# Hyena's filter weights as two diagonal blocks, one matmul for both halves of the positions

## The chip, the cores and the metric

The kernel runs on one core of one Trainium2 chip. The metric is the device time of one execution in microseconds (us). The kernel before takes 1653.63 us, the median of 3 runs that lie between 1647.57 and 1656.79 us.

## The reference, cut to what matters

The program is one layer of an encoder on 1024 positions of width 1024: RMSNorm, a projection whose columns feed four mixers (retention, a Mamba-2 state-space mixer, Hyena, gated DeltaNet), an output projection, a mixture of 16 experts, a gate and a final norm. The change lies in Hyena's long filters. A small network gives each of the L = 1024 positions 64 hidden values; its last layer maps these to 512 channels, 256 of the forward and 256 of the backward filter, and each channel is multiplied with its decay:

```python
def hyena_filters(L, w_in, b_in, w_mid, b_mid, freq, w_out):
    ...
        h = jnp.sin(freq * (h @ w_mid[j] + b_mid[j]))
    h = h @ w_out
    ...
    h = h * (jnp.exp(-t * jnp.abs(deltas)) + HY_SHIFT)
...
f_f = jnp.fft.rfft(filt, n=2 * L, axis=0)
```

The filters then go through a discrete Fourier transform, and the spectra are multiplied with those of the Hyena values.

## The kernel before

**Stages.** The first mixer stage projects the normalised input into the columns of the four mixers (matmuls L318 and L300, issued as fp32 split into a high and a low part), runs the gated DeltaNet's triangular inverses (`gdn_inverse`, VectorE lines L652 and L654 in 30 steps, then one ScalarE copy L657 and a store to DRAM, L658) and its scan (`gdn_scan`), and computes Hyena's filters and their transforms (`hy_transforms`). The scan fetches the stored inverses (L700) before its first matmuls (L714, L717), works on with L731, L744 and L761, and keeps its small evacuations on ScalarE. Later stages hold the other mixers, the output projection and the experts.

**Hyena's filters.** `hid` holds the hidden values (index 0 forward, index 1 mirrored for the backward filter): the 64 of the first half of the positions on partitions 0 to 63, those of the second half on partitions 64 to 127. `hy_transforms` goes through four quarters of 64 channels. In each it loads the weights `wo` (both halves' partitions get the same 64 rows, by GpSimd's queue, L1153), the decay `S` (L1154) and the bias (L1155). Then for each half `h` of the positions it makes eight matmuls with contraction 64 and 64 moved columns into the PSUM tile `tk`, of which there is one buffer, and VectorE multiplies the 128x512 results with the decay (L1166). In fp32 each matmul is issued as two passes, so a half is 16 passes in the trace, a quarter 32, the whole 128. After the second half, GpSimd adds the bias (L1168), forms sum and difference (L1170, L1171), ScalarE copies (L1172), and `dft16` makes a 16-point transform out of GpSimd additions (L1208) and ScalarE scalings (L1209); a store of the spectra (L1175) ends the quarter. A second loop of four quarters loads the Hyena values (L1180), runs `dft16` on them and stores (L1183). All tiles are slices of the two buffers `prm` and `prr`.

**Order.** The generators of these parts are woven into each other:

```python
weave((self.gdn_inverse(), 10), (islice(rest, 40), 40), (islice(tf, 6), 6))
weave((self.gdn_scan(), 48), (rest, 88), (tf, 14))
```

Here `rest` are the remaining projections and `tf` is `hy_transforms`. This is the order in the program's text only: the framework's scheduler, which works from modelled times of each instruction, sets the order in which each engine gets its instructions. The filters' matmuls are held behind the last projection matmul issued so far (`self.after(self.on_pj.ins)`). An engine works through its own list in order. The projections' convolution tile `cin` has its edges cleared by GpSimd (L335, L336), in the same list as the additions of `dft16`.

Of the kernel before, what the change touches and what calls it, by code (L numbers as in the profile page):

```python
# [14 lines left out]
OP = mybir.AluOpType  # L15
# [833 lines left out]
class Mix:  # L849
# [288 lines left out]
    def hy_transforms(self):  # L1138

        nc, a = self.nc, self.a  # L1140
        room = self.t1([128, 2432], "prm")
        z = room[:, 1024:2048].rearrange("p (a b) -> p a b", a=16)
        w = self.t1([128, 768], "prr").rearrange("p (a b) -> p a b", a=12)

        S = room[:, 0:1024].rearrange("p (i t c) -> p i t c", i=2, t=8)
        wo = room[:, 2048:2176].rearrange("p (i c) -> p i c", i=2)
        bi = room[0:1, 2176:2240]
        cols = lambda x: x.rearrange("p (i c) -> p i c", i=2)
        dec = a["c_fdec"].rearrange("(t p) (i c) -> i p t c", p=128, i=2)
        for q in range(4):  # L1150
            qs = slice(q * 64, q * 64 + 64)
            for h in range(2):
                nc.gpsimd.dma_start(wo[h * 64:h * 64 + 64], cols(a["hy_filt_w_out"][0])[:, :, qs])  # L1153
                nc.sync.dma_start(S[:, h], dec[h][:, :, qs])  # L1154
            nc.sync.dma_start(bi, a["hy_bias"][:, qs])  # L1155
            yield
            for h in range(2):
                sl = slice(h * 64, h * 64 + 64)
                ph = self.p([128, 2, 4, 64], "tk", 1)
                with self.after(self.on_pj.ins):  # L1160
                    for t in range(4):
                        for i in range(2):
                            nc.tensor.matmul(ph[:, i, t], lhsT=self.hid[sl, i, t * 128:t * 128 + 128], rhs=wo[sl, i],
                                             start=True, stop=True)
                v = S[:, :, h * 4:h * 4 + 4]
                nc.vector.tensor_tensor(out=v, in0=ph, in1=v, op=OP.mult)  # L1166

            nc.gpsimd.tensor_tensor(out=S[0:1, 0, 0], in0=S[0:1, 0, 0], in1=bi, op=OP.add)  # L1168

            nc.gpsimd.tensor_tensor(out=w[:, 0:8], in0=S[:, 0], in1=S[:, 1], op=OP.add)  # L1170
            nc.gpsimd.tensor_tensor(out=S[:, 1], in0=S[:, 0], in1=S[:, 1], op=OP.subtract)  # L1171
            nc.scalar.copy(S[:, 0], w[:, 0:8])  # L1172
            yield
            self.dft16(S[:, 0], S[:, 1], lambda i: z[:, i], w)
            nc.gpsimd.dma_start(self.ZF[:, :, qs], z)  # L1175
            yield
        for q in range(4):
            qs = slice(q * 64, q * 64 + 64)
            x = room[:, (q % 2) * 512:(q % 2) * 512 + 512].rearrange("p (t c) -> p t c", t=8)
            nc.sync.dma_start(x, self.HV[:, :, qs].rearrange("t p c -> p t c"))  # L1180
            yield
            self.dft16(x, x, lambda i: z[:, i], w)
            nc.sync.dma_start(self.ZX[:, :, qs], z)  # L1183
            yield
# [1059 lines left out]
```

## Time and profile before

| what | value |
|---|---|
| median of 3 runs | 1653.63 us |
| the profiled execution | 1651.48 us |
| its span, first to last instruction | 1649.6 us |
| mean granted TensorE clock | 0.959 |
| TensorE matmuls (PE) busy | 1513.7 us, 92% |
| VectorE (DVE) busy | 1195.3 us, 72% |
| ScalarE (ACT) busy | 862.2 us, 52% |
| GpSimd (POOL) busy | 559.0 us, 34% |
| chain that ended last | PE 45%, DMA 18%, DVE 17%, issue 8%, POOL 6%, ACT 5% |

Busy shares are of the span. The chain is followed back from the last instruction, at each step to what released it. Times in rows count from the span's start, and the profiled execution is 1.9 us longer than its span. A bracket such as `[2.47 <-ACT mo L922]` at the end of a row says how long the engine was idle before the instruction and which instruction ended that. PE is TensorE's matmuls, PEld its weight loads, SP the engine that issues most transfers (SPq is its queue).

### The profile page before, as it was taken

To read this page: it belongs to the slowest core of one execution; us is meant where nothing else is said; L and a number is where in the kernel's file an instruction comes from. 1 tells how busy PE (TensorE), PEld (TensorE's weight loads), DVE (VectorE), ACT (ScalarE), POOL (GpSimd) and SP (SyncE) were. 2 spreads that over 40 slices of the span, in tenths; PEclk is the share of its full clock that TensorE was granted. 3 is DMA by queue.
4 is the path that set the end of the run, shared out by engine and by line. 5 is a ranking of instruction groups with operands and counts; after the bars stand their busy time and mean duration, and the time that the engine had idled before them with its cause. 6 is when DMAs were issued, how large, how long until landed. Compare 5 with 4: busy or idle time off the path is not lost.

```text
span 1649.6 us, 25979 instructions
## 1 busy us (share of the span) xinstructions
PE 1513.7 (92%) x9148; PEld 1251.9 (76%) x9148; DVE 1195.3 (72%) x2060; ACT 862.2 (52%) x1413; POOL 559.0 (34%) x778
## 2 busy tenths in 40 slices
PE   4999999999999899779997999999898999999997
PEld 4877778988778776568875787886676688787886
DVE  5589876942556477955778797998888887777673
ACT  6255342123444335433223776887776767676662
POOL 3126665672865068462223110111111021121121
PEclk9999999999999899869997999999999999999999
DMA  5213557454545485154345999999999988888771
GB/s 182 61 39 96 168 155 243 131 161 105 166 122 167 139 288 163 55 181 156 135 154 214 359 337 363 317 339 350 349 355 336 348 294 295 293 310 303 236 276 52
DMA packets 200671, 362.53 MB, mean 220 GB/s; under 512 B 62046, under 2 KB 124732, under 8 KB 200285
## 3 DMA queue, kind: packets, MB, share of 16 engines
q1 hardware_dynamic: 169016, 296.13, 52.2%
q0 software_dynamic: 12400, 42.29, 8.5%
q10 hardware_dynamic: 19125, 22.45, 4.0%
q8 instruction: 72, 1.18, 0.3%
q14 instruction: 58, 0.48, 0.1%
HBM read 301.04 MB, written 59.77 MB: 219 GB/s over the span
## 4 chain that ended last, share of the span: by engine, by line
PE 45%; DMA 18%; DVE 17%; issue 8%; POOL 6%; ACT 5%; SPq 0%; POOLq 0%; ACTq 0%; DVEq 0%
PE pj L300 8%; DVE wl L1622 6%; PE pj L318 5%; PE ga L1646 4%; DMA raw<-in_exp_w_gate_dram 4%; PE ga L1648 4%; PE ga L1647 4%; DMA raw<-in_exp_w_up_dram 3%; ACT wh L1620 2%; POOL prm L1208 2%; POOL prr L1208 2%; PE pj L1647 2%; PE pj L1646 2%; PE pj L1648 2%; DMA RT<-mo 2%
## 5 line engine op out<-in xcount | busy, mean ns | idle before, releaser
L1622 DVE TENSOR_TENSOR wl<-raw,wh 128x1024 fp32r<-128x1024 f32 x340 | 408.3, 1223 | 86.2 <-ACT wh L1620 83.6
L1620 ACT CAST wh<-raw 128x1024 fp32r<-128x1024 f32 x344 | 356.4, 1052 | 139.1 <-DMA raw<-in_exp_w_up_dram 46.1
L1647 PE MATMUL ga<-wl,xh 128*128 128x512 f32 x512 | 206.4, 403 | 6.8 <-DVE wl L1622 6.7
L1648 PE MATMUL ga<-wh,xl 128*128 128x512 f32 x480 | 189.8, 396 | 0.0
L1646 PE MATMUL ga<-wh,xh 128*128 128x512 f32 x480 | 177.2, 407 | 10.0 <-ACT wh L1620 9.7
L1647 PEld LDWEIGHTS ga<-wl,xh 128*128 128x128 f32 x512 | 98.1, 192 | 34.7 <-DVE wl L1622 15.9
L318 PE MATMUL pj<-wh,hnh 128*128 128x256 f32 (+1 forms) x384 | 113.0, 295 | 7.9 <-DVE zss L915 4.6
L300 PE MATMUL pj<-hnh,wh 128*128 128x512 f32 x288 | 118.4, 411 | 0.8 <-ACT cin L337 0.8
L1646 PEld LDWEIGHTS ga<-wh,xh 128*128 128x128 f32 x480 | 90.6, 191 | 34.9 <-ACT wh L1620 16.5
L300 PE MATMUL pj<-hnl,wh 128*128 128x512 f32 x288 | 117.0, 406 | 0.0
L2009 POOL DMA_INDIRECT H<-b,pidx x15 | 35.4, 2357 | 240.6 <-ACT b L2008 213.7
L300 PE MATMUL pj<-hnh,wl 128*128 128x512 f32 x288 | 116.7, 405 | 0.0
L318 PE MATMUL pj<-wl,hnh 128*128 128x256 f32 (+1 forms) x384 | 110.5, 288 | 0.0
L318 PE MATMUL pj<-wh,hnl 128*128 128x256 f32 (+1 forms) x384 | 110.5, 288 | 0.0
L1647 PE MATMUL pj<-wl,hh 128*128 128x512 f32 x256 | 103.8, 406 | 4.1 <-DVE wl L1622 4.1
L1648 PEld LDWEIGHTS ga<-wh,xl 128*128 128x128 f32 x480 | 91.8, 191 | 18.1
L1648 PE MATMUL pj<-wh,hl 128*128 128x512 f32 x256 | 100.1, 396 | 0.0
L1956 POOL DMA_INDIRECT a<-HN,pidx x16 | 29.9, 1871 | 200.0 <-PE pj L1647 66.4
L1646 PE MATMUL pj<-wh,hh 128*128 128x512 f32 x256 | 89.9, 397 | 0.2 <-ACT hh L1636 0.2
L318 PEld LDWEIGHTS pj<-wh,hnh 128*128 128x128 f32 x384 | 74.4, 194 | 10.4 <-issue 4.1
L346 DVE SCALAR_TENSOR_TENSOR cacc<-cin,pcolh,cacc 128x1024 f32<-128x1024 f32 x48 | 64.8, 1349 | 15.6 <-POOL prm L1208 7.0
L318 PEld LDWEIGHTS pj<-wl,hnh 128*128 128x128 f32 x384 | 74.3, 193 | 0.5 <-issue 0.3
(540 smaller groups left out, 3751.6 us busy)
## 6 DMA issues: line engine op xcount, KB each, us to landing
raw<-in_exp_w_down_dram SPq DMA_DIRECT2D x128, 512.0 KB
raw<-in_exp_w_gate_dram SPq DMA_DIRECT2D x108, 512.0 KB
raw<-in_exp_w_up_dram SPq DMA_DIRECT2D x104, 512.0 KB
wraw<-in_w_in_dram SPq DMA_DIRECT2D x30, 512.0 KB
g<-WD SPq DMA_DIRECT2D x16, 768.0 KB
room<-in_exp_w_up_dram SPq DMA_DIRECT2D x24, 512.0 KB
WD<-gB SPq DMA_DIRECT2D x16, 640.0 KB
room<-in_exp_w_gate_dram SPq DMA_DIRECT2D x18, 512.0 KB
```

The costliest lines, as they stand in the source:

```text
L300: self.on_pj = nc.tensor.matmul(pj, lhsT=A[:, kt], rhs=B[:, kt, hs], start=i == 0, stop=i == 23)
L318: self.on_pj = nc.tensor.matmul(pj, lhsT=A[:, kt, ts], rhs=B[:, kt, :], start=i == 0, stop=i == 23)
L346: nc.vector.scalar_tensor_tensor(acc, cin[:, 2 - r + j:2 - r + j + 1024], w[j], acc, op0=OP.mult, op1=OP.add)
L1208: tt = lambda o, a, b, op: nc.gpsimd.tensor_tensor(out=o, in0=a, in1=b, op=op)
L1620: nc.scalar.copy(h, r)
L1622: e.tensor_tensor(out=l, in0=r, in1=h.bitcast(F32), op=OP.subtract)
L1646: nc.tensor.matmul(ps, lhsT=xh[:, k], rhs=wh[:, hs], start=first, stop=False)
L1647: nc.tensor.matmul(ps, lhsT=xh[:, k], rhs=wl[:, hs], start=False, stop=False)
L1648: return nc.tensor.matmul(ps, lhsT=xl[:, k], rhs=wh[:, hs], start=False, stop=last)
L1956: self.fetched = self.nc.gpsimd.indirect_dma_start(out=xg, out_offset=None, in_=self.HN if src is None else src, in_offset=bass.IndirectOf ...
L2009: nc.gpsimd.indirect_dma_start(out=self.H, out_offset=bass.IndirectOffsetOnAxis(ap=idx[:, :1], axis=0), in_=y, in_offset=None, compute_op= ...
```

## The change

The weights `wo` become two diagonal blocks on 128 partitions: rows 0 to 63 feed the columns of the first half, rows 64 to 127 those of the second, and the off-diagonal blocks are zeroed once by two GpSimd memsets of 64x2x64 (L1152 after the change). A matmul then contracts over all 128 partitions and moves 128 columns, and gives both halves of the positions for 128 positions at once. The loop over the halves `h` becomes one over `n`, the pairs of position tiles: per `n` four matmuls (8 passes) instead of eight (16 passes). The layout of `tk` is one PSUM bank as before; the product with the decay is done in two VectorE operations of 128x2x2x64 (128x256) instead of one of 128x512. Names: L1163 is L1165 after the change, L1166 is L1169; the other lines of the function after them move by 3.

```diff
+        wo = room[:, 2048:2304].rearrange("p (i h c) -> p i h c", i=2, h=2)
+        bi = room[0:1, 2304:2368]
+        for h in range(2):
+            nc.gpsimd.memset(wo[h * 64:h * 64 + 64, :, 1 - h], 0.0)
...
-                nc.gpsimd.dma_start(wo[h * 64:h * 64 + 64], cols(a["hy_filt_w_out"][0])[:, :, qs])
+                nc.gpsimd.dma_start(wo[h * 64:h * 64 + 64, :, h], cols(a["hy_filt_w_out"][0])[:, :, qs])
...
-            for h in range(2):
-                sl = slice(h * 64, h * 64 + 64)
-                ph = self.p([128, 2, 4, 64], "tk", 1)
+            for n in range(2):
+                ph = self.p([128, 2, 2, 2, 64], "tk", 1)
                 with self.after(self.on_pj.ins):
-                    for t in range(4):
+                    for t in range(2):
                         for i in range(2):
-                            nc.tensor.matmul(ph[:, i, t], lhsT=self.hid[sl, i, t * 128:t * 128 + 128], rhs=wo[sl, i],
-                                             start=True, stop=True)
-                v = S[:, :, h * 4:h * 4 + 4]
-                nc.vector.tensor_tensor(out=v, in0=ph, in1=v, op=OP.mult)
+                            nc.tensor.matmul(ph[:, i, t], lhsT=self.hid[:, i, (2 * n + t) * 128:(2 * n + t) * 128 + 128],
+                                             rhs=wo[:, i], start=True, stop=True)
+                v = S.rearrange("p i (h t) c -> p i t h c", h=2)[:, :, 2 * n:2 * n + 2]
+                for i in range(2):
+                    nc.vector.tensor_tensor(out=v[:, i], in0=ph[:, i], in1=v[:, i], op=OP.mult)
```

The scheduler's order moves with it. On VectorE, at the end of the inverses (L652 and L654 are their last steps; L1166 and L1169 the third quarter's products with the decay; L926 a projection's product), the order before was:

```order
L652 TENSOR_TENSOR gB<-gB,g_2541 128x2x30
L654 TENSOR_TENSOR gB<-gB 128x2x30
L285 TENSOR_TENSOR wl<-wraw,wh 128x1024
L1166 TENSOR_TENSOR prm<-tk,prm 128x2x256
L926 SCALAR_TENSOR_TENSOR mo<-zss,pj 128x256
L1166 TENSOR_TENSOR prm<-tk,prm 128x2x256
```

and now it is:

```order
L285 TENSOR_TENSOR wl<-wraw,wh 128x1024
L652 TENSOR_TENSOR gB<-gB,g_2541 128x2x30
L1169 TENSOR_TENSOR prm<-tk,prm 128x2x2x64 x2
L654 TENSOR_TENSOR gB<-gB 128x2x30
L926 SCALAR_TENSOR_TENSOR mo<-zss,pj 128x256
L1169 TENSOR_TENSOR prm<-tk,prm 128x2x2x64 x2
```

The last step of the inverses now stands behind the third quarter's first products, which wait for their matmuls. On ScalarE, the copy of the finished inverses (L657), which the store L658 waits for, stood before among the projections' evacuations (L922, L925) like this:

```order
L922 COPY mo<-pj 128x256
L928 DMA RT<-mo 128x256
L657 COPY gB<-gB 128x32x32
L922 COPY mo<-pj 128x256
L284 CAST wh<-wraw 128x1024
L928 DMA RT<-mo 128x256
L925 ACTIVATE zss<-pj 128x256
```

and now like this:

```order
L922 COPY mo<-pj 128x256
L284 CAST wh<-wraw 128x1024
L928 DMA RT<-mo 128x256
L925 ACTIVATE zss<-pj 128x256
L657 COPY gB<-gB 128x32x32
L928 DMA RT<-mo 128x256
```

The copy has moved behind an evacuation, a cast and the first L925. On TensorE, at the fourth quarter's matmuls in the scan (L1163, L1165 after the change; the L7xx are the scan's, L300 the projections'), the order before was, from the quarter's first matmuls on:

```order
L1163 MATMUL tk<-prm,hid 128x64 x3
L761 MATMUL sp<-gB,g_3419 128x64 x4
L1163 MATMUL tk<-prm,hid 128x64 x2
L714 MATMUL ga<-gB 32x32 x8
L717 MATMUL ga<-gB 32x32
L761 MATMUL sp<-gB,g_3419 128x64 x4
L717 MATMUL ga<-gB 32x32 x7
L1163 MATMUL tk<-prm,hid 128x64 x3
L717 MATMUL ga<-gB 32x32 x8
```

with the second half's matmuls eleven rows further on; now it is:

```order
L1165 MATMUL tk<-prm,hid 128x128 x4
L761 MATMUL sp<-gB,g_3408 128x64 x4
L717 MATMUL ga<-gB 32x32 x16
L761 MATMUL sp<-gB,g_3408 128x64 x4
L1165 MATMUL tk<-prm,hid 128x128 x4
```

The two groups of the quarter, which before were spread over the scan's matmuls and eight projection matmuls, now stand close together.

## Rows read from the trace of the kernel before

**Rows 1.** Busy time by stretch; columns are named in the first line.

```profile
core 0: us, PE busy (x) PEld busy (x) DVE busy (x) ACT busy (x) POOL busy (x), PEclk, DMA share, GB/s
300.00:320.00 20.00, 17.71 (x147) 16.99 (x147) 19.15 (x46) 1.06 (x1) 8.88 (x17) 1.00 0.45 120
340.00:365.00 25.00, 24.92 (x204) 24.17 (x204) 6.35 (x14) 6.20 (x11) 15.37 (x35) 0.94 0.68 222
348.00:353.00 5.00, 5.00 (x42) 4.80 (x42) 2.22 (x3) 1.03 (x2) 0.92 (x2) 1.00 1.02 372
365.00:397.00 32.00, 32.00 (x398) 28.24 (x397) 9.55 (x17) 14.55 (x47) 13.96 (x36) 1.00 0.54 143
440.00:460.00 20.00, 17.87 (x132) 14.92 (x132) 8.97 (x12) 9.00 (x26) 14.92 (x36) 0.91 0.59 168
480.00:500.00 20.00, 16.82 (x155) 13.88 (x154) 8.87 (x12) 8.13 (x24) 15.02 (x33) 0.91 0.36 95
500.00:520.00 20.00, 17.59 (x134) 13.87 (x133) 12.51 (x16) 7.48 (x19) 14.33 (x26) 1.00 0.52 145
```

**Rows 2.** Chain of waits, 330 to 360: start, us, what.

```profile
340.08 8.62 PE pj L318 x60
348.70 1.93 PE tk L1163 x16
350.63 3.38 PE pj L318 x27
354.01 1.93 PE tk L1163 x16
355.93 4.08 PE pj L318 x33
```

**Rows 3.** Line L1163: count, duration ns min/median/max, first and last start.

```profile
L1163 PE MATMUL tk<-prm,hid x128: 272/272/472, 270.4 to 411.1; 64*128 64x64 f32 x128
```

**Rows 4.** Timeline, TensorE, 645 to 655: start, us, engine, line, tiles, count.

```profile
648.60 0.66 PE L1032 MATMUL ga<-sxb 128*128 128x128 f32 x4
649.10 1.03 PE L1035 MATMUL ga<-sST,sxb 128*128 128x256 f32 x4
```

**Rows 5.** Line L1166: count, duration ns min/median/max, first and last start.

```profile
L1166 DVE TENSOR_TENSOR prm<-tk,prm x8: 673/691/692, 275.6 to 411.5; 128x512 f32<-128x512 f32 x8
```

**Rows 6.** Timeline, a VectorE product from PSUM and a GpSimd memset.

```profile
313.38 0.42 DVE L912 TENSOR_TENSOR mo<-pj,rrot 128x256 f32<-128x256 f32 x1 [0.51 <-DMA RT<-mo]
361.60 0.68 POOL L758 MEMSET gB<- 64x256 f32 x2
```

**Rows 7.** Timeline 340 to 372, the inverses' last step, their copy and the scan's start.

```profile
342.35 0.36 DVE L654 TENSOR_TENSOR gB<-gB 128x60 f32<-128x60 f32 x1
345.27 2.09 ACT L657 COPY gB<-gB 128x1024 f32<-128x1024 f32 x1 [0.40 <-ACT mo L922]
347.38 0.32 SPq L658 DMA_DIRECT2D RA<-gB  x1
352.28 0.38 ACT L925 ACTIVATE zss<-pj 128x256 f32<-128x256 f32 x1 [3.63 <-PE pj L318]
358.00 0.35 SPq L700 DMA_DIRECT2D gB<-RU  x1
362.77 0.43 PE L714 MATMUL ga<-gB 32*32 32x32 f32 x8
```

**Rows 8.** Timeline 330 to 345, ScalarE's wait and TensorE's behind it.

```profile
338.20 1.57 ACT L1209 ACTIVATE prr<-prr 128x64 f32<-128x64 f32 x6 [3.74 <-POOL prr L1208]
340.08 0.58 PE L318 MATMUL pj<-wh,hnh 128*128 128x256 f32 x1 [2.47 <-ACT mo L922]
```

**Rows 9.** Timeline 390 to 420, the fourth quarter's matmuls and GpSimd.

```profile
397.10 0.88 PE L1163 MATMUL tk<-prm,hid 64*128 64x64 f32 x6
404.15 0.31 POOL L1168 TENSOR_TENSOR prm<-prm 1x64 f32<-1x64 f32 x1 [19.12 <-DVE prm L1166]
409.42 2.00 PE L1163 MATMUL tk<-prm,hid 64*128 64x64 f32 x16
```

**Rows 10.** Timeline 470 to 530, ScalarE and TensorE in the tail of the scan.

```profile
486.00 0.26 ACT L1209 ACTIVATE prr<-prr 128x64 f32<-128x64 f32 x1 [7.21 <-POOL prr L1208]
491.12 1.14 PE L717 MATMUL ga<-gB 32*32 32x32 f32 x32 [3.18 <-ACT gB L720]
```

More of the change, by code (lines that the diff above doesn't have):

```diff
@@ L1145, in hy_transforms @@
         S = room[:, 0:1024].rearrange("p (i t c) -> p i t c", i=2, t=8)
-        wo = room[:, 2048:2176].rearrange("p (i c) -> p i c", i=2)
-        bi = room[0:1, 2176:2240]
+        wo = room[:, 2048:2304].rearrange("p (i h c) -> p i h c", i=2, h=2)
+        bi = room[0:1, 2304:2368]
         cols = lambda x: x.rearrange("p (i c) -> p i c", i=2)
         dec = a["c_fdec"].rearrange("(t p) (i c) -> i p t c", p=128, i=2)
+        for h in range(2):
+            nc.gpsimd.memset(wo[h * 64:h * 64 + 64, :, 1 - h], 0.0)
         for q in range(4):
```

## The prediction

> **What bounds the kernel now.** I read the shares of the whole span first: TensorE is busy for 92% of it and holds 45% of the chain, so time saved on TensorE can count, but only where TensorE is what ends last. So next the busy time by stretch, over the part that holds the filters. From 300 to 320 VectorE works 19.15 of 20 us and TensorE 17.71: VectorE, with the inverses and the evacuations, is the bound [rows 1]. From 340 to 397 TensorE has 24.92 of 25 and 32.00 of 32 us: it is the bound, and a pass removed there is time [rows 1]. The chain agrees: from 340.08 to past 355.93 it is nothing but projection matmuls and two groups of the filter [rows 2]. In the tail of the scan TensorE idles again: 20 − 17.87, 20 − 16.82 and 20 − 17.59 make 7.7 us, and in two of these stretches the granted clock is 0.91 [rows 1]. The filter's matmuls run from 270.4 to 411.1 in eight groups of 16 passes [rows 3]: four of them by 320, four from 348.70 on [rows 2].
>
> **What goes: half of the passes.** A group of 16 passes with 64 moved columns takes 1.93 us, 0.121 each [rows 2]. The new group has 8 passes of 128x128 weights with 128 moved columns. The same shape runs in the second stage: four passes from 648.60 until the next line starts at 649.10, 0.50 us, or 0.124 each [rows 4]. So a new group should take 8 × 0.124 = 0.99 and saves 0.94. By the busy time of the same row, 0.66 for four, it would be 1.32 and save 0.61. From below, no saving at all (a rival, below). I take 0.94, since the start of the next line is when the engine was free. The four early groups lie where VectorE is the bound, so I count 0 for them (at most −3.8). The four late ones are on the path: 4 × 0.94 = **−3.8** (−2.4 by the dearer price).
>
> **What is added.** VectorE: one product of 128x512 takes 0.69 us [rows 5]; of the new 128x256 ones the nearest row is a product out of PSUM of that size, 0.42 [rows 6]. Two make 0.84, so +0.15 for each of eight, 1.2 in all. The late four are covered by a VectorE that works 6.35 of 25 us and 9.55 of 32 [rows 1]; the early four are not, 0.6. GpSimd: the two memsets of 64x256 at 361.60 took 0.34 each [rows 6]; the new ones write half as much, before the filters' first loads, where nothing of the filter has begun: they cost 0 unless GpSimd is late there, 0.7 if it is. Loads are the same in number and bytes. Together I take **+0.5** (0 to 1.3).
>
> **What is moved: the start of the scan.** Before, the inverses' last step ends at 342.35 + 0.36 = 342.7, their copy runs from 345.27 to 347.4, the store goes out at 347.38, the first fetch at 358.00, and the scan's first matmul is at 362.77 [rows 7]. In the new order on VectorE the last L654 stands behind the third quarter's products, which wait for a group that TensorE began at 348.70 [rows 2]. On ScalarE the copy now stands behind the first L925, which waited 3.63 us for its projection and began at 352.28 [rows 7]. With one group 0.94 shorter ahead of it, L925 begins at 351.3 and ends at 351.7, and the copy ends at 353.8. (The last L654 is done by then: group at 348.70 + 0.99, 0.84 for the products, 0.36, so 350.9.) The store is thus 353.8 − 347.4 = 6.4 us later than before. Behind the copy in ScalarE's list stand the transfers and evacuations of the projections, 2.09 us each time they are due in that moment; two PSUM buffers cover that.
>
> What does TensorE do meanwhile? The order gives it 26 more projection matmuls before the scan's first one. Such matmuls take 4.08/33 = 0.124 [rows 2], so 3.2 us; two shorter groups give back 1.9. It comes to the scan's first matmul at 362.77 + 3.2 − 1.9 = 364.1. The fetched inverses: before, it took 358.00 − 347.38 = 10.6 us from the store to the first fetch, and 4.8 more to the matmul [rows 7]. If both stay, the data is there at 353.8 + 15.4 = 369.2, and TensorE waits 5.1. But the store went out into a stretch where the transfers' share was 1.02, their engines full [rows 1]; later it competes with fewer, and with 6 instead of 10.6 the wait is 0.5. Between 0.5 and 5.1 I take **+3**, nearer to the row than to the hope.
>
> **What is moved: the second quarter.** Before 340.08 TensorE idled 2.47 us for an evacuation by ScalarE, which had itself waited 3.74 us for GpSimd's additions of the transform [rows 8]. VectorE now reaches the second quarter's last product two places earlier in its list, so these additions start earlier. The wait goes, or stays: between −2.5 and 0, and I take **−1**; the same chain of GpSimd and ScalarE is the next thing late there.
>
> **What is moved: the fourth quarter.** Before, its matmuls began at 397.10 and the second group ended at 409.42 + 2.00 = 411.4, with the scan's matmuls and eight projections in between; GpSimd idled 19.12 us for the first product and could form the sum only after the second [rows 9]. Now both groups stand together, so that GpSimd begins up to 411.4 − 397.1 − 3 = some 11 us earlier (3 us for the two groups and the scan's matmuls between them). GpSimd's transforms are late in the tail: there ScalarE stands 7.21 us behind the additions (L1209 waits for L1208), and TensorE 3.18 for an evacuation that ScalarE owes the scan [rows 10]. If that goes, TensorE wins the 7.7 us of idle time and what the clock lost: 0.91 over 20 us is 1.8 us lost in each of two stretches (the mean between the level of 2.4 GHz and that of 1.2, after TensorE had paused), 3.6 in all. So between 0 and −11.3. But the scaling stays ahead of the scan's evacuations in ScalarE's list, the transforms of the second loop keep their number, and the scan itself starts later, so the collision is shifted more than removed. I take **−3**, a quarter.
>
> **Sum.** −3.8 + 0.5 + 3 − 1 − 3 = −4.3. The profiled execution took 1651.5 us, which gives 1647.2. The median of the runs shown is 2.1 above it, so I forecast 1653.6 − 4.3 = **1649.3**. All later stages stand as before, since their instructions are the same.
>
> **Rivals.**
> B, the tail is freed: the early fourth quarter takes all of the 11.3 away. For it: the idle time of GpSimd before 404.15. Against it: the same additions, in the same number, still compete for ScalarE. −3.8 + 0.5 + 3 − 1 − 11.3 = −12.6, so 1641.0.
>
> C, the scan waits, and the kernel is slower: the copy behind the first L925 makes TensorE wait the whole 5.1 us at the scan's first matmul. After that pause the clock falls as in the tail, 1.8 more, and the next fetches are late by 0.9 (between the scan's first groups now stand seven projection matmuls fewer, 7 × 0.124). Nothing is won at the second quarter or in the tail. −3.8 + 0.5 + 5.1 + 1.8 + 0.9 = +4.5, so 1658.1; with waits in the tail that grow by as much as the start is late, up to 1664. For it: the orders on both engines, and a path that in the rows took 15.4 us. Against: the full queues at that moment. It decides against me once store to fetch takes 9 us or more.
>
> D, no saving on TensorE: the time of a pass goes with its moved columns, so that 8 × 128 cost what 16 × 64 did. Then −3.8 falls away: −0.5, so 1653.1. Against it: 0.121 at 64 columns and 0.124 at 128 [rows 2, 4]. The Trainium skill ("TensorE: Matmul & The Clock Gate", section "Back-to-back issue gap") has a rule of this kind: its table gives about 60 cycles for a matmul of up to 64 moved columns and 134 for one of 128, so that by an estimate from it 16 passes cost 960 cycles and 8 cost 1072, and the change would win nothing. Rows 2 and 4 of this case differ from it: the passes stand 0.121 and 0.124 us apart, far over both figures. The same page ("LDWEIGHTS (loading the stationary operand)") says that a weight load takes its time by its columns and not by the contraction, by which the fuller contraction is free; the trace agrees in so far as the pass with all 128 rows is no dearer.
>
> **How the numbers follow.** Chances: forecast 0.47, B 0.23, C 0.25, D 0.05. The forecast's own range is 1641 to 1658, from its bounds (tail −8 to 0, start +0.5 to +5.1). What this measurement can tell from no change is about 0.5%, 8.3 us: faster is below 1645.4, slower above 1661.9. Faster: 0.12 of the forecast's 0.47, 0.18 of B = 0.30. Slower: 0.01 of the forecast, 0.14 of C (its upper half), 0.01 of D = 0.16. The rest, 0.54, is no difference that can be told. The range reaches over most of B and C: 1637 to 1663.
>
> **What would show it.** The group of L1165 takes 1.0 us, not 1.9 (else D). The store of the inverses goes out near 353.8; the first L714 starts near 364 to 369 with TensorE idle 0.5 to 5 before it (over 5: C). The fourth quarter's sum on GpSimd starts near 401 instead of 412.33. Idle time of TensorE from 440 to 520 is 4 to 7 us and one of the dips of the clock is gone (none left: B). The forecast fails if the scheduler's other moves, in the convolution tiles and the second stage, cost or save more than these terms.

## The result: 1% faster, past the forecast

The changed kernel takes 1635.7 us (median of 6 runs, 1632.0 to 1641.3); the kernel before, on the same chip, 1653.3. The ratio is 0.990, 95% interval 0.9875 to 0.992, so some 17.5 us faster. The forecast was 1649.3 with a range of 1637 to 1663. The profiled executions are 1631.96 and 1651.48, the spans 1630.1 and 1649.6.

Nearly all of it is won in one place. Three parts of the first mixer stage, cut at the same projection matmuls in both kernels (the 793rd, the 1301st, and the 1537th, which is the first L300 of the last group), show it; the third part ends with the scan's last matmul. The kernel before, busy time by stretch:

```profile
core 0: us, PE busy (x) PEld busy (x) DVE busy (x) ACT busy (x) POOL busy (x), PEclk, DMA share, GB/s
255.60:341.10 85.50, 76.07 (x597) 73.40 (x597) 71.97 (x156) 17.10 (x37) 53.77 (x82) 0.95 0.56 171
341.10:383.10 42.00, 42.00 (x438) 39.80 (x438) 10.12 (x20) 14.50 (x39) 27.58 (x67) 0.98 0.63 185
383.10:564.20 181.10, 173.14 (x1629) 148.60 (x1627) 91.50 (x125) 73.29 (x190) 85.37 (x172) 0.96 0.44 125
```

The kernel after:

```profile
254.40:338.80 84.40, 71.94 (x565) 69.85 (x566) 68.89 (x152) 16.69 (x37) 52.79 (x82) 0.94 0.58 172
338.80:381.10 42.30, 39.52 (x366) 37.15 (x365) 10.45 (x26) 12.90 (x34) 29.13 (x69) 0.92 0.58 168
381.10:547.00 165.90, 165.66 (x1667) 142.84 (x1667) 94.75 (x131) 75.52 (x197) 72.14 (x172) 1.00 0.51 141
```

The first two parts hold six of the eight filter groups, and they take 127.5 us before and 126.7 after, a gain of only 0.8 us. TensorE does have less to do there: its busy time, less what the slow clock costs, falls from 113.0 to 102.9 us, by 48 passes and by 56 small matmuls of the scan, which now come behind the third cut (168 of the scan's stand ahead of it before, 112 after). But its idle time grows from 9.4 to 15.2 us, and the slow clock costs 8.5 us instead of 5.1. The third part, the tail of the scan, falls from 181.1 to 165.9 us. Before, TensorE idled 8.0 us in it and ran 13.7 us of it at 1.2 GHz, which costs 6.8 by an estimate (half of that time; the last section has the rows at either clock); after, it idles 0.2 us and the granted clock is 1.00 throughout. That is 14.5 of the 15.2.

The same numbers can be summed by kind and not by place: of the 16.0 us that the three parts win, 10.7 are work that is gone (the passes some 8 of it, by an estimate from 8 groups of 1.93 − 0.89), 1.9 idle time and 3.4 slow clock. So the saved work turns into waiting ahead of the tail, and in the tail waiting goes; what each would be worth alone is the question of the experiments.

From the end of the stage to the end of the run the kernel after takes 2.3 us less (1083.1 and 1085.4). Over the profiles of all fourteen kernels here that rest lies between 1081 and 1096 us, so I read nothing from the difference.

The terms one by one. Lines L1165 and L1169 (count, duration min/median/max, first and last start):

```profile
L1165 PE MATMUL tk<-prm,hid x64: 270/275/348, 269.5 to 394.2; 128*128 128x128 f32 x64
L1169 DVE TENSOR_TENSOR prm<-tk,prm x16: 406/416/426, 271.6 to 394.9; 128x256 f32<-128x256 f32 x16
```

The two new memsets, and TensorE's wait at the second quarter:

```profile
L1152 POOL MEMSET prm<- x2: 198/200/202, 262.8 to 263.0; 64x128 f32 x2
338.25 0.38 PE L318 MATMUL pj<-wh,hnh 128*128 128x256 f32 x1 [2.91 <-ACT mo L922]
```

The scan's start, by the chain of waits (start, us, what) and the timeline:

```profile
345.33 0.89 PE tk L1165 x8
346.22 1.43 PE pj L318 x12
347.65 0.02 issue
347.68 0.05 ACT zss L925
347.73 0.23 issue
347.96 2.10 ACT gB L657
350.06 0.02 issue
350.08 10.90 DMA RA<-gB
```

```profile
347.40 0.27 DVE L654 TENSOR_TENSOR gB<-gB 128x60 f32<-128x60 f32 x1
363.40 0.41 PE L714 MATMUL ga<-gB 32*32 32x32 f32 x8 [1.12 <-DMA gB<-RA]
```

On the chain a group now takes 0.89 instead of the 1.93 of [rows 2]. The last L654 ends at 347.7 instead of 342.7, the copy stands behind the first L925 as the order said, and TensorE waits 1.12 us at the scan's first matmul [rows 7]. In the tail, GpSimd's sum of the fourth quarter in the kernel before:

```profile
412.33 1.28 POOL L1170 TENSOR_TENSOR prr<-prm 128x512 f32<-128x512 f32 x1 [7.86 <-issue]
```

And the timeline of the kernel after on TensorE, GpSimd and ScalarE:

```profile
389.79 1.05 PE L1165 MATMUL tk<-prm,hid 128*128 128x128 f32 x8
393.37 1.11 PE L1165 MATMUL tk<-prm,hid 128*128 128x128 f32 x8
395.41 1.27 POOL L1173 TENSOR_TENSOR prr<-prm 128x512 f32<-128x512 f32 x1 [3.72 <-issue]
478.80 0.54 ACT L1212 ACTIVATE prr<-prr 128x64 f32<-128x64 f32 x2 [4.13 <-POOL prr L1211]
```

The fourth quarter's sum starts 17 us earlier (395.41 instead of 412.33), and ScalarE's longest wait for the additions falls from 7.21 [rows 10] to 4.13. In the kernel before, TensorE's waits in the tail ended mostly with ScalarE's evacuations (who waited for what; us in total, times, longest):

```profile
PE ga L717 <- ACT gB L720: 3.2, 1, 3.2
PE sp L761 <- DVE g L748: 2.4, 2, 1.4
PE ga L744 <- ACT gB L732: 2.1, 1, 2.1
```

In the kernel after only a wait of 0.2 is left. The last store of the second loop goes out at 490.7 instead of 522.4, so the chain of transforms has gained 31 us, 14 more than TensorE. What waits in SP's queue between 400 and 530 shows a second list that changes. Before:

```profile
SPq L1183 <- POOL prm L1208: 16.5, 2, 13.4
SPq L1180 <- POOL prr L1208: 10.0, 2, 8.6
SPq L1183 <- POOL cin L336: 8.9, 1, 8.9
```

After:

```profile
SPq L1186 <- POOL prm L1211: 8.0, 3, 3.4
SPq L1183 <- POOL prr L1211: 5.4, 3, 3.0
```

The store of a spectrum (L1183, L1186 after the change) or the load of the next values (L1180, now L1183) waits for GpSimd at the head of SP's queue, and behind it stand the scan's fetches (L700, L693) and the projections' weights (L282). Before, it held them up to 13.4 us at a time, now 3.4. That this list cost TensorE time in the kernel before is not shown: the rows above name ScalarE and VectorE. The prediction had read ScalarE's list in the tail, not SP's.

### The profile page after: what moved, and what is told of

It reads as the page before. It is cut to its first block, busy times and chain, and to the rows that moved or that the text cites. A ratio compares the mean times of both kernels' runs of the same rounds, so it can differ in the third digit from the quotient of the medians.

```text
span 1630.1 us, 25864 instructions
## 1 busy us (share of the span) xinstructions
PE 1494.8 (92%) x9084; PEld 1235.3 (76%) x9084; DVE 1200.2 (74%) x2068; ACT 860.4 (53%) x1413; POOL 558.2 (34%) x780
## 4 chain that ended last, share of the span: by engine, by line
PE 50%; DMA 19%; DVE 16%; issue 7%; ACT 5%; POOL 3%; SPq 0%; POOLq 0%; ACTq 0%; DVEq 0%
PE pj L300 12%; DVE wl L1625 5%; PE pj L318 5%; DMA raw<-in_exp_w_gate_dram 5%; PE ga L1649 5%; PE ga L1651 5%; PE ga L1650 5%; DMA raw<-in_exp_w_up_dram 3%; ACT wh L1623 2%; PE pj L1650 2%; PE pj L1651 2%; PE pj L1649 2%; PE sp L761 2%; DMA a<-H,tidx 1%; DMA raw<-in_exp_w_down_dram 1%
## 5 line engine op out<-in xcount | busy, mean ns | idle before, releaser
L318 PE MATMUL pj<-wh,hnh 128*128 128x256 f32 (+1 forms) x384 | 113.7, 297 | 13.4 <-DVE zss L915 8.6
L2012 POOL DMA_INDIRECT H<-b,pidx x15 | 39.3, 2617 | 238.4 <-ACT b L2011 169.0
L300 PE MATMUL pj<-hnh,wh 128*128 128x512 f32 x288 | 116.7, 405 | 0.8 <-ACT cin L337 0.8
L300 PE MATMUL pj<-hnh,wl 128*128 128x512 f32 x288 | 115.7, 402 | 0.0
L300 PE MATMUL pj<-hnl,wh 128*128 128x512 f32 x288 | 115.7, 402 | 0.0
L1959 POOL DMA_INDIRECT a<-HN,pidx x16 | 37.6, 2349 | 187.4 <-PE pj L1650 65.5
L318 PEld LDWEIGHTS pj<-wh,hnl 128*128 128x128 f32 x384 | 75.1, 196 | 0.7 <-issue 0.5
```

The costliest lines, as they stand in the source:

```text
L300: self.on_pj = nc.tensor.matmul(pj, lhsT=A[:, kt], rhs=B[:, kt, hs], start=i == 0, stop=i == 23)
L318: self.on_pj = nc.tensor.matmul(pj, lhsT=A[:, kt, ts], rhs=B[:, kt, :], start=i == 0, stop=i == 23)
L1959: self.fetched = self.nc.gpsimd.indirect_dma_start(out=xg, out_offset=None, in_=self.HN if src is None else src, in_offset=bass.IndirectOf ...
L2012: nc.gpsimd.indirect_dma_start(out=self.H, out_offset=bass.IndirectOffsetOnAxis(ap=idx[:, :1], axis=0), in_=y, in_offset=None, compute_op= ...
```

## The experiments

"Tail" is the part from the first L300 of the last group to the last scan matmul; its idle time and its loss to the clock (half of the time that the trace puts at 1.2 GHz) are from one profile each, the times from all runs, and ratios are to the kernel before on the same chip. The cut lies between 379 and 387 us, but at 393 in x1 and at 401 in x6, since more of the scan stands ahead of it there.

| kernel | median us | ratio, 95% | tail: idle + clock us | last store of spectra |
|---|---|---|---|---|
| before | 1651 to 1657 | 1 | 8.0 + 6.8 | 522 |
| after | 1635.7 | 0.990, 0.9875 to 0.992 | 0.2 + 0 | 491 |
| x1_two_products | 1657.2 | 1.0015, 1.000 to 1.003 | 7.8 + 3.4 | 521 |
| x2_one_product | 1639.5 | 0.991, 0.988 to 0.994 | 0.2 + 0 | 496 |
| x3_twice | 1649.4 | 0.997, 0.995 to 1.000 | 4.6 + 5.1 | 516 |
| x6_weave | 1647.0 | 0.996, 0.994 to 0.998 | 3.7 + 3.4 | 499 |
| x5_later4 | 1645.1 | 0.993, 0.9905 to 0.996 | 3.9 + 1.7 | 530 |
| x9_no_second | 1636.2 | 0.989, 0.9865 to 0.992 | 0.2 + 3.4 | 467 |
| x14_after_no_second | 1638.1 | 0.9885, 0.9855 to 0.991 | 0.2 + 0 | 455 |
| x10_inverse_first | 1645.5 | 0.994, 0.992 to 0.996 | 5.0 + 1.7 | 495 |
| x11_after_weave | 1644.4 | 0.993, 0.991 to 0.995 | 2.1 + 3.4 | 492 |
| x7_scale_pool | 1663.9 | 1.006, 1.0035 to 1.008 | 14.1 + 10.2 | 531 |
| x13_pool_queue | 1674.8 | 1.012, 1.009 to 1.014 | 13.9 + 20.5 | 552 |
| x15_three_cut | 1650.1 | 0.999, 0.998 to 1.000 | 0.2 + 6.8 | 545 |

**Which part of the change does it: x1, x2, x3.** In x1 the kernel before gets only the split product:

```diff
-                nc.vector.tensor_tensor(out=v, in0=ph, in1=v, op=OP.mult)
+                for i in range(2):
+                    nc.vector.tensor_tensor(out=v[:, i], in0=ph[:, i], in1=v[:, i], op=OP.mult)
```

> The kernel before with only VectorE's side of the change: two products of 128x256 per half instead of one of 128x512; matmuls as before. Theory (half the passes, and an earlier fourth quarter that frees the tail of the scan): nothing is gained, 1653 within 5, TensorE's idle time and slow clock from 400 to 520 stay at some 14 us together. Rival 1 (the split products and the order they bring free the tail): 1645 or less.

Measured: 1657.2, ratio 1.0015, idle time and slow clock of the tail 11.2 (a stretch of slow clock near 401, 3.4 in the kernel before, is missing). Nothing is gained, as the theory says. In x2 the kernel after loses the split and keeps the diagonal blocks:

```diff
-                            nc.tensor.matmul(ph[:, i, t], lhsT=...
+                            nc.tensor.matmul(ph[:, i, :, t], lhsT=...
...
-                v = S.rearrange("p i (h t) c -> p i t h c", h=2)[:, :, 2 * n:2 * n + 2]
-                for i in range(2):
-                    nc.vector.tensor_tensor(out=v[:, i], in0=ph[:, i], in1=v[:, i], op=OP.mult)
+                v = S.rearrange("p i (h t) c -> p (i h) (t c)", h=2)[:, :, 128 * n:128 * n + 128]
+                nc.vector.tensor_tensor(out=v, in0=ph.rearrange("p i h t c -> p (i h) (t c)"), in1=v, op=OP.mult)
```

> The kernel after with VectorE's split undone: the block-diagonal matmuls write PSUM in strides, and one product of 128x512 follows. Theory: the tail stays free, 1636 within 5, VectorE about 1 us less busy. Rival 1 (the split products free the tail): back to 1645 to 1650.

Measured: 1639.5, tail free. Rival 1 falls. In x3 every block-diagonal matmul is issued twice:

```diff
-                            nc.tensor.matmul(ph[:, i, t], lhsT=...
+                            for _ in range(2):
+                                nc.tensor.matmul(ph[:, i, t], lhsT=...
```

> The kernel after with each block-diagonal matmul issued twice, so that a group is 16 passes again (some 1.98 us); loads, products and layout as after. Theory: the passes' 4 to 8 us come back, the fourth quarter's groups are spread over the scan's matmuls again, and the tail idles again: 1648 to 1654. Rival 1 (grouping and products matter, not the passes): the tail stays free, only the passes come back, 1640 to 1645.

Measured: 1649.4, the last groups spread out again in the order, 9.7 us of idle time and slow clock back. So the gain goes with the length of the groups. As x3 also puts back the passes, some 8 us, it does not by itself divide the passes from the tail.

**Does an early fourth quarter free the tail: x6 and x5.** x6 is the kernel before with a larger share for the transforms in the weave:

```diff
-        weave((self.gdn_scan(), 48), (rest, 88), (tf, 14))
+        weave((self.gdn_scan(), 48), (rest, 88), (tf, 18))
```

> The kernel before, all its passes kept, with the transforms given a larger share in the second weave (18 instead of 14), so that the fourth quarter comes earlier in the program. Theory: the transforms end before the scan's evacuations need ScalarE, idle time and slow clock from 400 to 520 fall from 14 us to under 5, 1640 to 1646. Rival 2 (only the removed passes count, and what the tail lost was given by chance): no change, 1650 to 1656.

Measured: 1647.0, a ratio of 0.996, and 7.1 us left in the tail. Another 5.1 us of slow clock, from 388 to 398, lie just ahead of the cut of x6; with them 12.2 of 14.8 us are left, so that the idle time is halved and the slow clock has not shrunk. The direction of the theory, then, and less than half its size. With every pass kept, an earlier start alone gains 0.2 to 0.6%. x5 is the reverse, the kernel after with its fourth quarter held back:

```diff
             yield
+            if q == 3:
+                for _ in range(2):
+                    yield
             for n in range(2):
```

> The kernel after with the fourth quarter's matmuls held back by two turns of the weave: they stand behind 1638 projection matmuls instead of 1560 (some 18 us later), everything ahead of them as in the kernel after. Theory (the tail is free because the transforms end early): the transforms end near 510, TensorE's idle time and slow clock in the tail come back with 5 to 12 us, 1641 to 1648. Rival 2 (the passes count, the transforms' time does not): 1636 within 4.

Measured: 1645.1, 5.6 us back in the tail, the last store at 530. The longest wait is again for ScalarE's list: a scaling waits 8.06 us for GpSimd, a projection's L871 stands behind it and VectorE's L872 behind that, for which TensorE waits:

```profile
522.09 0.54 ACT L1215 ACTIVATE prr<-prr 128x64 f32<-128x64 f32 x2 [8.06 <-POOL prr L1214]
526.70 0.39 PE L318 MATMUL pj<-wh,hnh 128*128 128x256 f32 x1 [3.08 <-DVE zss L872]
```

Rival 2 falls: with all the saved passes in place, about half of the gain goes with the start of the fourth quarter alone.

**What is the change worth without the tail: x9 and x14.** In both the transforms of the Hyena values are left out (from the kernel before and after):

```diff
-            self.dft16(x, x, lambda i: z[:, i], w)
+            for g in range(2):
+                nc.gpsimd.tensor_copy(z[:, g * 8:g * 8 + 8], x)
```

> The kernel before with the transforms of the Hyena values left out (two copies by GpSimd in the place of each dft16 of the second loop); filters and scan as before. Theory: nothing of ScalarE's list waits for GpSimd in the tail, idle time and slow clock there under 3 us, 1638 to 1645. Rival 3 (the scan's own chain): they stay over 10, 1650 to 1657.

> The kernel after with the transforms of the Hyena values left out as in x9_no_second; the pair with x9_no_second (1636.2) shows what the change is worth where no transforms press on the tail. Theory (most of the change's 17 us is the tail of the kernel before): the two differ by 0 to 6 us, so 1630 to 1636. Rival 2 (the passes alone bring the 17): 1617 to 1622.

Measured: 1636.2 and 1638.1, ratios of 0.989 and 0.9885 with intervals that lie over each other. In x9, with all passes kept, the tail's idle time is gone (0.2 us), so these transforms are what made TensorE wait there; the slow clock near 401 stays (3.4). Without these transforms the change is worth nothing that can be told (some 7 us either way by the intervals). Where the saved passes go, the stretches of x9 and x14 up to the scan show. x9:

```profile
254.50:339.60 85.10, 72.92 (x598) 70.05 (x598) 71.63 (x155) 16.77 (x37) 53.35 (x80) 1.00 0.56 171
339.60:382.20 42.60, 42.60 (x438) 40.41 (x437) 10.52 (x21) 14.67 (x40) 27.80 (x68) 0.96 0.62 184
```

x14:

```profile
254.70:342.20 87.50, 71.49 (x565) 69.67 (x565) 72.26 (x152) 16.52 (x37) 50.68 (x82) 0.94 0.55 166
342.20:383.70 41.50, 38.45 (x366) 36.11 (x365) 10.33 (x26) 12.98 (x34) 29.06 (x69) 0.96 0.59 172
```

TensorE is busy 5.6 us less in x14 and idle 6.9 us more: in the first part it waits for VectorE, in the second for VectorE's L926 (1.34) and for the fetched inverses (1.14). As in the main pair, the saved work ahead of the tail turns into waiting; here the tail holds nothing to be won but the slow clock (3.4).

**Which waits carry the tail: x7, x13, x15.** x7 moves the scalings of the kernel before to GpSimd, so that none stands in ScalarE's list:

```diff
-        scaled = lambda o, a, s: nc.scalar.activation(o, a, AF.Copy, scale=s)
+        scaled = lambda o, a, s: nc.gpsimd.tensor_scalar(o, a, s, None, op0=OP.mult)
```

> The kernel before with the transforms' scalings on GpSimd instead of ScalarE; all passes and the fourth quarter's place kept. Theory (scalings that stand in ScalarE's list ahead of the scan's evacuations and wait for GpSimd make TensorE wait): idle time and slow clock in the tail fall from 14.8 to under 4 us, 1640 to 1646. Rival 3 (TensorE waits there for the scan's own chain over VectorE): they stay over 10, 1650 to 1657.

Measured: 1663.9, slower, and 24.3 us in the tail: a miss. TensorE's long wait there, what ScalarE waited for, and SP's queue:

```profile
522.23 0.66 PE L761 MATMUL sp<-gB,g 128*128 128x64 f32 x2 [11.44 <-DVE gq L766]
```

```profile
517.63 1.04 ACT L284 CAST wh<-wraw 128x1024 fp32r<-128x1024 f32 x1 [16.30 <-DMA wraw<-in_w_in_dram]
```

```profile
SPq L1180 <- POOL cin L336: 29.8, 2, 16.7
SPq L1183 <- POOL prm L1208: 26.7, 2, 13.8
```

ScalarE no longer waits for scalings; it waits for weights, whose load stands in SP's queue behind a store of spectra that waits for a GpSimd that now has more to do. So x13 takes the second loop's loads and stores out of SP's queue as well:

```diff
-            nc.sync.dma_start(x, self.HV[:, :, qs]...
+            nc.gpsimd.dma_start(x, self.HV[:, :, qs]...
...
-            nc.sync.dma_start(self.ZX[:, :, qs], z)
+            nc.gpsimd.dma_start(self.ZX[:, :, qs], z)
```

> The kernel before with the scalings on GpSimd (as in x7_scale_pool) and the second loop's loads and stores in GpSimd's queue as well, so that neither ScalarE's list nor SP's waits for the transforms; order on TensorE as in x7_scale_pool. Theory in its second form (late transforms reach TensorE over two lists, ScalarE's scalings and SP's stores with the weights and the scan's fetches behind them): idle time and slow clock in the tail fall from x7's 24 to under 6 us, 1642 to 1650. Rival 3 (the scan's own chain, or GpSimd's edges of the convolution tiles, set the tail): they stay over 15, 1655 to 1665.

Measured: 1674.8, a miss again. SP's queue waits for no transform any more, but ScalarE does, in a third way:

```profile
513.08 1.24 ACT L343 ACTIVATE cacc<-cin,pcolh 128x1024 f32<-128x1024 f32 x1 [8.84 <-POOL cin L336]
538.04 1.24 ACT L343 ACTIVATE cacc<-cin,pcolh 128x1024 f32<-128x1024 f32 x1 [9.68 <-POOL cin L336]
```

The edges of the convolution tiles, two memsets, stand in GpSimd's own list behind the additions. x15 is x13 with these edges cleared by VectorE in the tail:

```diff
-        nc.gpsimd.memset(cin[:, 2 - r:2], 0.0)
-        nc.gpsimd.memset(cin[:, 1026:1026 + r], 0.0)
+        edge = nc.vector if bias is not None and half else nc.gpsimd
+        edge.memset(cin[:, 2 - r:2], 0.0)
+        edge.memset(cin[:, 1026:1026 + r], 0.0)
```

> x13_pool_queue (the kernel before with scalings, loads and stores of the transforms on GpSimd) with the edges of the tail's convolution tiles cleared by VectorE instead of GpSimd, so that nothing of the scan or the projections stands behind the transforms in any list. All passes are kept. Theory in its third form (what stands behind the transforms in an engine's list is what makes TensorE wait): idle time and slow clock in the tail under 6 us, 1640 to 1650. Rival 3 (the scan's own chain over VectorE sets the tail): they stay over 15, 1658 to 1675.

Measured: 1650.1. By the ratios, each to the kernel before on its own chip, that is some 21 us less than x13, and no gain over the kernel before (0.998 to 1.000). Busy time by stretch of x13 and of x15:

```profile
480.00:520.00 40.00, 34.09 (x275) 27.93 (x275) 21.49 (x25) 12.25 (x23) 32.39 (x67) 0.93 0.44 131
520.00:560.00 40.00, 32.21 (x293) 29.54 (x290) 18.56 (x27) 10.21 (x23) 27.87 (x55) 0.77 0.34 103
```

```profile
400.00:440.00 40.00, 40.00 (x355) 33.46 (x355) 17.73 (x25) 16.53 (x38) 26.52 (x46) 0.87 0.39 110
480.00:520.00 40.00, 40.00 (x385) 34.23 (x380) 26.85 (x36) 18.60 (x40) 31.32 (x52) 1.00 0.41 125
```

With none of the three in the way TensorE is never idle in the tail, though all 128 passes are kept and the last store goes out at 545, 23 us later than in the kernel before. What made TensorE wait was thus not the transforms' end but the work that stood behind them in the lists of ScalarE, SP and GpSimd. The expectation holds for the idle time (0.2 us) and not for the clock: 6.8 us are lost between 392 and 414, where TensorE is busy throughout. The stage ends at 553.5, 10.7 us earlier than before, of which the whole run keeps nothing that can be told: the rest of the run takes 1094.3 us in this profile and 1085.4 in that of the kernel before. Why is not shown.

**Can more be had: x10 and x11.** x10 holds the third quarter's products of the kernel after behind the inverses' last step (`self.inv`, the last L654):

```diff
+                with self.after(self.inv.ins if q == 2 else None):
                     for i in range(2):
                         nc.vector.tensor_tensor(out=v[:, i], in0=ph[:, i], in1=v[:, i], op=OP.mult)
```

> The kernel after with the third quarter's products held behind the last step of the inverses on VectorE, which also brings the copy of the inverses ahead of the first L925 on ScalarE. Theory (the late inverses cost the idle time and slow clock at the scan's start, 6 us): 1629 to 1634, the tail stays free. Rival (the path from store to fetch sets the start in any case): 1636 within 3.

Measured: 1645.5, a miss. The scan's start kept its idle time (3.3 us, now a wait for VectorE's L926) and slow clock (3.4), and 5.0 us of idle time came back in the tail, although the transforms ended at 495 (491 in the kernel after). Some scalings had come further forward in ScalarE's list: those of the third transform stand behind 78 of the scan's evacuations and not behind 82. And ScalarE waits longer for GpSimd:

```profile
427.23 0.54 ACT L1213 ACTIVATE prr<-prr 128x64 f32<-128x64 f32 x2 [7.14 <-POOL prr L1212]
465.56 0.54 ACT L1213 ACTIVATE prr<-prr 128x64 f32<-128x64 f32 x2 [7.08 <-POOL prr L1212]
```

```profile
468.97 1.09 PE L744 MATMUL ga<-g,gB 64*64 64x128 f32 x16 [2.21 <-ACT gB L732]
```

So an early end of the transforms is not enough; their place in the other lists counts too. x11 gives the kernel after the weave of x6:

> The kernel after with the transforms' larger share in the second weave (18 instead of 14): fourth quarter behind 1512 projection matmuls instead of 1560, and the copy of the inverses ahead of the first L925. Theory: the tail is free already, so an earlier fourth quarter brings nothing there; at the scan's start up to 4 us are won: 1632 to 1637. Rival (each step earlier helps, as it did in x6_weave): 1625 to 1630.

Measured: 1644.4, below neither forecast, and by the ratios some 6 us slower than the kernel after, hardly clear of the intervals. None of these beats the kernel after.

## Why the prediction was wrong, point by point

- **The passes: right.** A group fell to 0.89 us on the chain (0.99 foretold; the rows are busy for 1.05 to 1.13), so rival D is out: twice the moved columns at half the passes halved the time. The Trainium skill's table behind D ("TensorE: Matmul & The Clock Gate", "Back-to-back issue gap") is given there for an isolated matmul. The passes here stand 0.12 and 0.11 us apart, and the estimate from that table does not hold for them. The early four groups brought little that lasts, as counted: TensorE's lead is 1.1 us at the first cut and 2.3 at the second.
- **VectorE and GpSimd: right in size.** A product takes 0.42 us, as read from the neighbouring row, and a memset 0.20.
- **The second quarter: nothing gone.** Counted −1; the wait of 2.47 us [rows 8] is now 2.91, for the same L922.
- **The scan's start: right for the wait, short for the clock.** Counted +3; TensorE idled 2.8 us in the second part, of which 1.1 was the wait for the inverses, and lost 3.4 instead of 0.9 to the clock, which was not counted. The copy began at 347.96, not at 351.7: L925 stands behind 12 projection matmuls after the group in both kernels, but the group itself began at 345.2 and not at the 348.70 that I had taken over, since TensorE was 3.5 us ahead there. And the transfer took 10.9 us from store to fetch; the 6 on which the lower bound stood did not come.
- **The tail: the step that failed.** "... so the collision is shifted more than removed. I take −3, a quarter." All of it was removed, idle time and slow clock. Rival B had the outcome, and at 0.23 too small a chance; of its mechanism, the earlier start, x5 shows about half. Its 11.3 were still short, since I had left out the slow clock from 400 to 440, where TensorE was not idle (0.91 over 40 us, 3.4 us). The measured 14.5 in place of 3 make up 11.5 of the 13 us by which the forecast missed. Ahead of the tail the terms came near: +0.6 counted (−1.9 for the third quarter, +0.5, +3 and −1), −0.8 measured.
- **Why it was misjudged.** I read the tail as one collision, ScalarE's scalings against the scan's evacuations, and took from it that the same work in the same lists must collide again. It can come about over three lists, and each is a matter of order: x9 and x14 show the change to be worth nothing that can be told where these transforms are gone, x15 shows the tail free of idle time with all passes kept.
- **The range.** The two bounds that it names (tail −8 to 0, start +0.5 to +5.1), with the other terms as counted, give 1641.8 to 1654.4 and not 1641 to 1658; its upper end also needs the dearer pass and the upper ends of the other terms.
- **What stays open.** How much of the tail comes from the earlier start and how much from the new order on ScalarE and SP. x5 puts about half on the start; x10 shows an order that undoes much of the gain at nearly the same start. Which of the lists weighed most in the kernel before was not tried one by one; 5.3 of its 8.0 us of idle time ended with ScalarE. And up to 3.4 of the 14.5 us, the slow clock near 401, may go with the form of the passes and not with the order (last section).

## What to carry to other kernels

Where an engine makes a long chain beside the critical path, look for everything of the critical path that stands behind that chain, in every engine's list and in the queues that issue its loads and stores: idle time there can go all at once. A scheduler that works from modelled times turns a small saving into another order, and the order may be worth as much as the saving or more, either way (x10 and x11 lost some 7 and 6 us, by their ratios, by edits that ought to have helped). So give the case in which such idle time vanishes whole a chance as large as that in which a part of it goes, and read every stretch with a low clock, those without idle time too.

## What the runs showed of the hardware

The granted clock fell to 1.2 GHz for 6.8 us from 401 in the kernel before while TensorE's rows show no idle time:

```profile
400.00:440.00 40.00, 40.00 (x351) 33.18 (x345) 17.61 (x21) 17.07 (x42) 21.87 (x40) 0.91 0.39 109
```

and in the kernel after it did not:

```profile
400.00:440.00 40.00, 40.00 (x427) 33.18 (x422) 24.77 (x29) 22.86 (x61) 28.11 (x68) 1.00 0.65 177
```

What the lower clock costs, the same six passes of the filter show: 0.88 us at 397.10, before the fall [rows 9], and 1.54 in it:

```profile
401.81 1.54 PE L1163 MATMUL tk<-prm,hid 64*128 64x64 f32 x6
```

Before the fall TensorE was at the scan's 32x32 matmuls and the filter's 64-row ones. It cost 3.4 us, as much as a wait of that length, and no list of waits names it. At the fourth quarter's matmuls, with no idle time of TensorE in the 12 us before it, such a fall stands in the profiles of six of the seven kernels with the 64-row passes (all but x1), for 3.4 to 17.1 us in all, and in none of the seven with the 128-row ones, x3 with its 16 passes a group included. That is one profile of each kernel. I had not expected it, and what brought it about was not tried.
